# Strassen's method in the down product of an MLP: seven products of quadrants for eight

## The chip, the cores and the metric

One core of one Trainium2 chip. The program is a single launch of one kernel; the metric is its device time in microseconds, and the times shown are those of whole executions. The kernel before took 2549.54, 2552.10 and 2552.34 us in three runs, median 2552.1 us. A profile was taken of one more execution.

## The reference

The reference is two transformer blocks one after the other, for 1024 tokens of width 1024, all in float32. The first block is a mixer (gated convolution and retention), a cross attention on 256 memory rows, and an MLP with a squared ReLU; the second has its own modulation vectors, a windowed attention with a short convolution, and a layer of 16 experts. The change concerns the MLP of the first block:

```python
def sq_relu_mlp(h, up_w, down_w):
    return jnp.square(jax.nn.relu(h @ up_w)) @ down_w     # (1024x1024 @ 1024x4096), then @ 4096x1024
...
h = h + sq_relu_mlp(rmsnorm(h, norm_mlp_w), mlp_up_w, mlp_down_w)
return rmsnorm(h, norm_f_w).astype(x.dtype)
```

and, because it fills gaps in the same stage, the modulation of the second block, `silu(c) @ w_ada + b_ada`: two rows (`c`, and `c_ctx` for a third of the columns) times a 1024x6144 matrix.

## The kernel before

Every large product is made of three matmuls: each float32 operand is split into a high part, rounded to the matmul's own float32r format, and a low part, the difference, and high x high, high x low and low x high are added up in PSUM (`mm3`, L143 to L145). A weight unit is 128x1024 (512 KB). `wunits` (L129) loads it from HBM into one of three `raw` buffers, and `split` (L117) has ScalarE copy the high part (L118) and VectorE subtract the low part (L119) into one of five `W` buffers. These loads and splits are written with a high priority, 1500 instructions ahead of their place.

The framework orders the instructions of each engine when the kernel is built: the written order ranks them, `high_priority` moves a rank forward, and an instruction whose operands come later by the framework's own estimate is passed over for one further back. The result is a fixed queue per engine, which the engine then works off in order, with semaphores between the engines. A tile with a tag (`R16`, `T6`, `W2`, `B4`) can be taken only when all readers of the tile before it with that tag are done.

The MLP (L771 on) runs over nine chunks of the 4096 hidden columns, of 2, 2 and seven times 4 blocks of 128 columns (`MLP_CHUNKS`). In a chunk, each up block is computed for both halves of 512 tokens (`fm_block`, 8 x 3 matmuls of 128x512 into one PSUM bank), ScalarE applies `relu` and `square`, and VectorE makes the high part (a cast) and the low part of `uT`. Then the down product of the chunk: for each of two column halves `nb` and eight token tiles `t`, `tm_block` adds up 4 x 3 matmuls in one of five banks (`pm`), and VectorE adds the bank to `acc[t]`, which holds the residual in SBUF (L801). The units of the down weights, four to a chunk, are the quadrants of its 512x1024 block: 256 rows by 512 columns each.

`mod_blocks` (L760) computes the modulation on VectorE: each of 48 blocks loads 512 KB of `w_ada` into the single buffer R32 and multiplies and sums it against rows of `crow` that are kept in T4 to T7, in two operations, or in four for the first 16 blocks, which use the rows in T6 and T7 as well. Eight blocks are written after each of the chunks 1 to 6. After the MLP, R32 takes `norm_f_w` (`wf`, L819), the sums are added to `modT` (L822), and the eight tiles of `acc` are normalised, tile by tile in the order in which the last chunk finishes them.

Of the kernel before, what the change touches and what calls it, by code (L numbers as in the profile page):

```python
# [11 lines left out]
F32R = mybir.dt.float32r  # L12
# [3 lines left out]
AF = mybir.ActivationFunctionType  # L16
# [2 lines left out]

EPS = 1e-6  # L20
MLP_CHUNKS = [2, 2] + [4] * 7
D = 1024
S = 1024
HALF = 512
# [10 lines left out]
def tile_kernel(ctx: ExitStack, tc: tile.TileContext, d, out, stop=None, dbg=None):  # L35
    nc = tc.nc
    pe, act, dve, pool = nc.tensor, nc.scalar, nc.vector, nc.gpsimd
# [3 lines left out]
    sb = ctx.enter_context(tc.tile_pool(name="sb", bufs=1))  # L41
# [12 lines left out]
    def nm(s):  # L54
        cnt[0] += 1
        return f"{s}_{cnt[0]}"
# [3 lines left out]
    def R(i, shape, dt=F32, name="r"):  # L60
        return sb.tile(shape, dt, tag=f"R{i}", bufs=1, name=nm(name))

    def T(i, shape, dt=F32, name="t"):
        return sb.tile(shape, dt, tag=f"T{i}", bufs=1, name=nm(name))

    def B(i, name="b"):
        return ps[0].tile([128, 512], F32, tag=f"B{i}", bufs=1, name=nm(name))
# [49 lines left out]
    def split(hi, lo, src):  # L117
        act.activation(hi, src, AF.Copy)  # L118
        dve.tensor_sub(lo, src, hi.bitcast(F32))  # L119

    raw_ring = [Ring([("raw", i) for i in range(3)])]
    w_ring = [Ring(range(5))]

    def raw_unit(src):
        pre, i = raw_ring[0]()
        raw = sb.tile([128, 1024], F32, tag=f"{pre}{i}", bufs=1, name=nm("raw"))
        nc.sync.dma_start(raw, src)
        return raw

    def wunits(src, i0, n, ahead=1500):  # L130

        res = []
        with tc.high_priority(offset=ahead):
            for u in range(i0, i0 + n):
                raw = raw_unit(src[u])
                w = sb.tile([128, 2, 1024], F32R, tag=f"W{w_ring[0]()}", bufs=1, name=nm("w"))
                split(w[:, 0, :], w[:, 1, :], raw)
                res.append(w)
        return res
# [18 lines left out]
    def fm_block(p, unit, rhs, n=512):  # L158

        for k in range(8):  # L160
            mm3(p[:, :n], (unit[:, 0, k * 128:(k + 1) * 128], unit[:, 1, k * 128:(k + 1) * 128]),
                rhs(k), k == 0, k == 7)
# [26 lines left out]
    def row_rstd(x):  # L189
        return rsqrt_of(sumsq(x), 1.0 / D)  # L190

# [6 lines left out]
    def unit_tiles(xs):  # L198
# [3 lines left out]
        for j, x in enumerate(xs):  # L202
            if j % 2 == 0:
                act.activation(junk, x, AF.Square, accum_out=ss[:, j:j + 1])
            else:
                dve.tensor_tensor_reduce(out=junk2, in0=x, in1=x, op0=OP.mult, op1=OP.add, scale=1.0, scalar=0.0,
                                         accum_out=ss[:, j:j + 1])
        r = rsqrt_of(ss, 1.0 / D, n)
        for j, x in enumerate(xs):
# [101 lines left out]
    def half_of(hT, half):  # L311
        def f(k):
            h = hT[half][k]
            return (h[:, 0, :], h[:, 1, :])
        return f

    def rows(t, n=1):
        return slice(t * 128, (t + n) * 128)
# [83 lines left out]
    for c in range(4):  # L402
        ub, ua = wunits(d["w_in_fm"], 2 * c, 2)
        for half in range(2):
            sl = slice(half * HALF, (half + 1) * HALF)
            p = B(pm(), "cb")
# [3 lines left out]
            p = B(pm(), "ca")  # L410
# [20 lines left out]
    uni = wunits(d["w_in_tm"], 4, 4)  # L431
    for t in range(8):
        p = B(pm(), "qk")
# [17 lines left out]
    uni = wunits(d["w_in_tm"], 8, 4)  # L451
# [168 lines left out]
    for h in range(4):  # L620
        uni = wunits(d["xk_fm"], 2 * h, 2)
        p = B(pmem(), "km")
# [5 lines left out]
    for nb in range(2):  # L628
        uni = wunits(d["xv_tm"], 4 * nb, 4)
        for j in range(2):  # L630
            p = B(pmem(), "vm")
# [106 lines left out]
    hm = {}  # L738
# [7 lines left out]
    acc = [load(R(24 + t, [128, 1024], name="acc"), h2_d[rows(t), :]) for t in range(8)]  # L746
# [13 lines left out]
    def mod_blocks(b0, n):  # L760

        for b in range(b0, b0 + n):
            raw = load(R(32, [128, 1024], name="wada"), d["w_ada"][b])
            for o in range(2 if b < 16 else 1):
                for h in range(2):
                    dve.tensor_tensor_reduce(out=mjunk, in0=raw[:, h * 512:(h + 1) * 512], in1=crow[o, h],  # L766
                                             op0=OP.mult, op1=OP.add, scale=1.0, scalar=0.0,
                                             accum_out=mpart[:, h, 48 * o + b:48 * o + b + 1])
# [1 line left out]
    rr = Ring([0, 1])  # L770
    rv = Ring([2, 3])  # L771
    UT = {0: [16, 21, 22, 23], 1: [17, 18, 19, 20]}
    ch0 = 0
    for ch, fbs in enumerate(MLP_CHUNKS):
        uT = {0: [], 1: []}
        for fb in range(fbs):
            uni = wunits(d["up_fm"], ch0 + fb, 1)
            for half in range(2):
                p = B(pm(), "up")
                fm_block(p, uni[0], half_of(hm, half))  # L780
                r = T(rr(), [128, 512], name="relu")
                act.activation(r, p, AF.Relu)  # L782
                v = T(rv(), [128, 512], name="sq")
                act.activation(v, r, AF.Square)
                ut = R(UT[half][fb], [128, 2, 512], F32R, name="uT")
                dve.tensor_copy(ut[:, 0, :], v)
                dve.tensor_sub(ut[:, 1, :], v, ut[:, 0, :].bitcast(F32))  # L787
                uT[half].append(ut)
        nu = fbs // 2
        if ch < 8:  # L790
            order = [(nb, t) for nb in range(2) for t in range(8)]
        else:
            order = [(nb, t) for t in range(8) for nb in range(2)]
        uni = {}
        for nb, t in order:
            if nb not in uni:
                uni[nb] = wunits(d["down_tm"], ch0 + nb * nu, nu)
            sl = slice(nb * 512, (nb + 1) * 512)
            p = B(pm(), "dn")
            tm_block(p, tile_of(uT, t), uni[nb])  # L800
            dve.tensor_add(acc[t][:, sl], p, acc[t][:, sl])  # L801
        ch0 += fbs
        if 1 <= ch < 7:
            mod_blocks(8 * ch - 8, 8)

# [20 lines left out]
    p = B(pt(), "modT")  # L828
# [8 lines left out]
    for t in range(8):  # L837
        x = acc[t]
        dbg_store("h3", (rows(t), slice(0, 1024)), x)
        s1 = sumsq(x)  # L840
        dve.tensor_mul(x, x, wf)
        s2 = sumsq(x)
        r = rsqrt_of(s1, 1.0 / D)
        q2 = tiny([128, 1])
        dve.tensor_mul(q2, r, r)
        dve.tensor_mul(q2, q2, s2)
        r2 = rsqrt_of(q2, 1.0 / D)
        r3 = tiny([128, 1])
# [107 lines left out]
    def attention(t):  # L956
# [16 lines left out]
        for kv in range(2):  # L973
            Pl = []
            for hp in range(2):
# [3 lines left out]
                for jj in range(2):  # L979
                    h = h0 + jj  # L980

                    s2 = ps[0].tile([128, 1024], F32, tag=f"D{jj}", bufs=1, name=nm("s2"))
                    pc, pl, sc = s2[:, 256:512], s2[:, 512:512 + nl], s2[:, 256:512 + nl]
# [54 lines left out]
    for c in range(4):  # L1038
        uni = wunits(d["w_in2_fm"], 3 * c, 3)
        uc = R(16, [128, 1024], name="u2")  # L1040
        yc = R(17, [128, 1024], name="y2")
        for half in range(2):
            sl = slice(half * HALF, (half + 1) * HALF)
            g = T(8, [128, 512], name="cg")
            p = B(pmc(), "cg")
# [3 lines left out]
            p = B(pmc(), "hv")  # L1049
# [8 lines left out]
        for half in range(2):  # L1058
            sl = slice(half * HALF, (half + 1) * HALF)
            p = B(pmc(), "bg")  # L1060
# [19 lines left out]
    p = B(7, "lb")  # L1080
# [103 lines left out]
    p = B(7, "aT")  # L1184
# [7 lines left out]
    src = p[:48, :]  # L1192
    for r in range(16):
        sl = slice(8 * r, 8 * r + 8)
        dve.max(G[:, sl], src)
        dve.max_index(Iu[:, sl], G[:, sl], src)
        if r < 15:
            dve.match_replace(out=aT, in_to_replace=G[:, sl], in_values=src, imm_value=-1.0)
            src = aT
# [8 lines left out]
    p = B(4, "GT")  # L1208
# [28 lines left out]
    for e in range(16):  # L1237
# [3 lines left out]
        for nb in range(2):  # L1241
            sl = slice(nb * 512, (nb + 1) * 512)
# [5 lines left out]
            p = B(pga(), "ga")  # L1248
# [5 lines left out]
            p = B(pga(), "up")  # L1254
# [11 lines left out]
        for nb in range(2):  # L1266
            sl = slice(nb * 512, (nb + 1) * 512)
# [7 lines left out]
    sq = tiny([128, 1])  # L1275
# [6 lines left out]
    for t4 in (0, 4):  # L1282
# [3 lines left out]
        r = rsqrt_of(ss, 1.0 / D, 4)  # L1286
# [3 lines left out]
    with tc.high_priority(offset=1500):  # L1290
        ss = tiny([128, 2])
        for nb in range(2):
            sl = slice(nb * 512, (nb + 1) * 512)
# [67 lines left out]
def layout(inputs):  # L1361
# [34 lines left out]
    chunks, r0 = [], 0  # L1396
    for fbs in MLP_CHUNKS:
        chunks.append(_tm(dn[r0:r0 + fbs * 128], [0, 512]))
# [38 lines left out]
```

## Time and profile before

| | before |
|---|---|
| three runs, us | 2549.54, 2552.10, 2552.34; median 2552.1 |
| the profiled execution, us | 2549.31 |
| its span, us | 2547.5 |
| mean granted TensorE clock | 0.983 |
| TensorE busy, us (share) | 2426.0 (95%) |
| VectorE busy, us (share) | 1774.4 (70%) |
| ScalarE busy, us (share) | 1172.0 (46%) |

The span is the time from the first to the last instruction of the profiled execution. Busy time is the union of an engine's instructions. The matmuls overlap: a 128x512 matmul is shown as 389 ns long, and the distance from one start to the next tells the pace. PE is TensorE, PEld its weight loads, DVE VectorE, ACT ScalarE, SP the engine that issues the loads and stores.

### The profile page before, as it was taken

What the parts mean: (1) busy time and instruction counts of PE and PEld (TensorE: products, weight loads), DVE (VectorE), ACT (ScalarE), POOL (GpSimd) and SP (SyncE); (2) the same over time, 40 slices, a digit from 0 to 9 for tenths busy, and PEclk for the clock granted to TensorE, in tenths of its full rate; (3) what the DMA queues carried; (4) which work ended last, traced back from release to release, by engine and by line L of the source; (5) the groups of instructions that cost most, each with busy time, mean ns of one, the idle gap of its engine ahead of it and who ended that gap; (6) DMA issues with size and microseconds to landing.
All of it is one profiled execution on the core that took longest, in us unless ns stands there. A gap on an engine that the chain in (4) does not pass through costs nothing.

```text
span 2547.5 us, 31406 instructions
## 1 busy us (share of the span) xinstructions
PE 2426.0 (95%) x11471; PEld 1971.0 (77%) x11471; DVE 1774.4 (70%) x3121; ACT 1172.0 (46%) x1791; POOL 56.5 (2%) x37
## 2 busy tenths in 40 slices
PE   7999899999999999999999999999994999999995
PEld 6887678888878888888888777777773888888774
DVE  6999883655477555333335858776558999999887
ACT  6113652544442122112214625554333888887775
POOL 0000000000000000000000000000000100011100
PEclk9999999999999999999999999999996999999998
DMA  4333545434443344211111221114674999999994
GB/s 177 101 127 114 167 162 194 142 99 162 133 166 121 119 149 149 71 42 50 58 49 70 98 79 50 38 54 145 206 268 147 389 396 394 393 394 388 361 375 157
DMA packets 138475, 442.79 MB, mean 174 GB/s; under 512 B 15664, under 2 KB 20176, under 8 KB 138320
## 3 DMA queue, kind: packets, MB, share of 16 engines
q1 hardware_dynamic: 133568, 423.48, 46.7%
q0 software_dynamic: 4752, 17.30, 2.7%
q8 instruction: 90, 1.47, 0.2%
q14 instruction: 65, 0.53, 0.1%
HBM read 388.28 MB, written 52.45 MB: 173 GB/s over the span
## 4 chain that ended last, share of the span: by engine, by line
PE 83%; DVE 7%; DMA 4%; ACT 3%; issue 2%; SPq 0%; DVEq 0%; POOLq 0%; ACTq 0%
PE up L144 6%; PE up L145 6%; PE up L143 6%; PE dn L144 6%; PE dn L145 6%; PE dn L143 6%; PE wo L143 3%; PE wo L144 3%; PE wo L145 3%; PE ga L144 2%; PE ga L145 2%; PE ga L143 2%; PE q L145 2%; PE q L144 2%; PE q L143 2%; DMA raw<-experts 2%
## 5 line engine op out<-in xcount | busy, mean ns | idle before, releaser
L118 ACT ACTIVATE w<-raw 128x1024 fp32r<-128x1024 f32 x560 | 584.6, 1058 | 742.4 <-PE dn L145 290.0
L119 DVE TENSOR_TENSOR w<-raw,w 128x1024 fp32r<-128x1024 f32 x560 | 673.0, 1222 | 183.0 <-ACT w L118 171.5
L143 PE MATMUL dn<-w,uT 128*128 128x512 f32 x512 | 199.6, 390 | 0.7 <-ACT relu L782 0.5
L143 PE MATMUL up<-hm,w 128*128 128x512 f32 x512 | 199.7, 390 | 0.0
L144 PE MATMUL up<-hm,w 128*128 128x512 f32 x512 | 199.4, 390 | 0.0
L145 PE MATMUL up<-hm,w 128*128 128x512 f32 x512 | 199.4, 389 | 0.0
L144 PE MATMUL dn<-w,uT 128*128 128x512 f32 x512 | 199.2, 389 | 0.0
L145 PE MATMUL dn<-w,uT 128*128 128x512 f32 x512 | 198.8, 390 | 0.0
L801 DVE TENSOR_TENSOR acc<-dn,acc 128x512 f32<-128x512 f32 x144 | 97.9, 687 | 91.5 <-PE dn L145 91.1
L766 DVE CUSTOM_DVE_ANT_0 mws<-wada,crow 128x512 bf16<-128x512 f32 x128 | 88.2, 689 | 104.4 <-DMA wada<-w_ada 102.3
L423 DVE SCALAR_TENSOR_TENSOR y<-u,small,y 128x1023 f32<-128x1023 f32 (+25 forms) x120 | 145.8, 1261 | 0.4
L143 PEld LDWEIGHTS dn<-w,uT 128*128 128x128 f32 x512 | 96.1, 188 | 21.8 <-ACT relu L782 1.2
L145 PEld LDWEIGHTS dn<-w,uT 128*128 128x128 f32 x512 | 96.0, 188 | 20.5 <-DVE uT L787 0.6
L145 PEld LDWEIGHTS up<-hm,w 128*128 128x128 f32 x512 | 96.1, 188 | 20.0
L144 PEld LDWEIGHTS up<-hm,w 128*128 128x128 f32 x512 | 96.1, 188 | 19.8
L144 PEld LDWEIGHTS dn<-w,uT 128*128 128x128 f32 x512 | 96.1, 188 | 19.8
L143 PEld LDWEIGHTS up<-hm,w 128*128 128x128 f32 x512 | 96.0, 188 | 19.8 <-ACT hm L228 0.3
L144 PE MATMUL ga<-w,x1T 128*128 128x512 f32 x256 | 101.7, 397 | 1.7 <-DVE w L119 1.7
L144 PE MATMUL dn<-w,x1T 128*128 128x512 f32 x256 | 101.4, 396 | 2.0 <-DVE w L119 2.0
L143 PE MATMUL dn<-w,x1T 128*128 128x512 f32 x256 | 102.4, 401 | 0.5 <-ACT w L118 0.5
L145 PE MATMUL dn<-w,x1T 128*128 128x512 f32 x256 | 101.2, 395 | 0.0
L145 PE MATMUL ga<-w,x1T 128*128 128x512 f32 x256 | 101.1, 395 | 0.0
(435 smaller groups left out, 5453.2 us busy)
## 6 DMA issues: line engine op xcount, KB each, us to landing
raw<-experts SPq DMA_DIRECT2D x384, 512.0 KB, 7.1
wada<-w_ada SPq DMA_DIRECT2D x48, 512.0 KB, 3.5
raw<-up_fm SPq DMA_DIRECT2D x32, 512.0 KB, 4.2
raw<-down_tm SPq DMA_DIRECT2D x32, 512.0 KB, 4.4
raw<-w_out_tm SPq DMA_DIRECT2D x24, 512.0 KB, 4.3
raw<-w_in_fm SPq DMA_DIRECT2D x20, 512.0 KB, 3.9
h_d<-hx SPq DMA_DIRECT2D x32, 256.0 KB, 2.9
raw<-xq_fm SPq DMA_DIRECT2D x16, 512.0 KB, 5.0
```

Source lines behind the costliest of these rows:

```text
L118: act.activation(hi, src, AF.Copy)
L119: dve.tensor_sub(lo, src, hi.bitcast(F32))
L143: pe.matmul(out_, l[0], r[0], start=first, stop=False)
L144: pe.matmul(out_, l[0], r[1], start=False, stop=False)
L145: pe.matmul(out_, l[1], r[0], start=False, stop=last)
L423: dve.scalar_tensor_tensor(yc[:, s:], uc[:, :1024 - s], convw[:, c, 30 - s:31 - s], yc[:, s:], op0=OP.mult, op1=OP.add)
L766: dve.tensor_tensor_reduce(out=mjunk, in0=raw[:, h * 512:(h + 1) * 512], in1=crow[o, h], op0=OP.mult, op1=OP.add, scale=1.0, scalar=0.0, a ...
L801: dve.tensor_add(acc[t][:, sl], p, acc[t][:, sl])
```

## The change

The six chunks 2 to 7 no longer multiply the four quadrants of their activations (512 tokens by 256 hidden columns each) with the four quadrants of their down weights in eight products, but form seven products of sums and differences of quadrants, in Winograd's variant of Strassen's method. Each product is 512x256 times 256x512: four banks of six matmuls. The sums that several results share are not formed again: a product is added in PSUM to the four banks that hold the one before, and VectorE adds the banks to `acc` at each stage of their growth, four adds to a quadrant of the result; there are seven such groups of four.

The chunks 0, 1 and 8 keep the old form, which moves into a function `mlp_chunk`. In the new `mlp_chunk_7` the up blocks come in two groups of four, with the first product between them. The quadrants of activations and their sums are held in R16 to R23 and in W3 and W4; the ring of weight buffers is cut to three in these chunks. The squares go to T0 to T3 in the first group and to T6 and T7 in the second. The up blocks use the banks 4 to 7, the products banks 0 to 3 (`bA`, `bC`) and 4 to 7 (`bB`). The sums of weight quadrants (T1 to T4 of the method) are formed on VectorE in the raw buffers, in place, ahead of their place by a priority of 1500; the first quadrant of the weights is loaded twice. The modulation blocks are spread anew: eight after each of the chunks 0 and 1, five after each of the chunks 2 to 7, two after the last.

```diff
 MLP_CHUNKS = [2, 2] + [4] * 7
+MOD_BLOCKS = [8, 8] + [5] * 6 + [2]
...
+    pu = Ring([4, 5, 6, 7])
+    def x_place(i, name):
+        if i < 4:
+            return [R(16 + 2 * i + f, [128, 2, 512], F32R, name=name) for f in range(2)]
+        w = sb.tile([128, 2, 2, 512], F32R, tag=f"W{i - 1}", bufs=1, name=nm(name))
+        return [w[:, 0], w[:, 1]]
+    def mlp_chunk_7(ch0):
+        def u_block(unit, half, place):
+            p = B(pu(), "up")
+            fm_block(p, unit, half_of(hm, half))
+            v = T(place, [128, 512], name="sq")
+            act.activation(v, p, AF.Relu)
+            act.activation(v, v, AF.Square)
+            return v
+        def put(op, v):
+            split(op[:, 0, :], op[:, 1, :], v)
...
+        def product(bank, op, w, first):
+            for j in range(4):
+                for f in range(2):
+                    o = f * 512
+                    l0, l1 = op[f][:, 0, rows(j)], op[f][:, 1, rows(j)]
+                    r0, r1 = w[:, 0, o:o + 512], w[:, 1, o:o + 512]
+                    for i, (l, r) in enumerate(((l0, r0), (l0, r1), (l1, r0))):
+                        pe.matmul(bank[j], l, r, start=first and f + i == 0, stop=f == 1 and i == 2,
+                                  skip_group_check=not first)
+        def add(bank, half, nb):
+            sl = slice(nb * 512, (nb + 1) * 512)
+            for j in range(4):
+                a = acc[4 * half + j]
+                dve.tensor_add(a[:, sl], bank[j], a[:, sl])
+        xA, xB = x_place(0, "x11"), x_place(1, "s3")
+        s3, x21 = [], []
+        for f in range(2):
+            uni = wunits(d["up_fm"], ch0 + f, 1)
+            a = u_block(uni[0], 0, 2 * f)
+            put(xA[f], a)
+            b = u_block(uni[0], 1, 2 * f + 1)
+            dve.tensor_sub(a, a, b)
+            put(xB[f], a)
+            s3.append(a)
+            x21.append(b)
+        w = wunits(d["down_tm"], ch0, 1)[0]
+        bA = [B(j, "dnA") for j in range(4)]
+        product(bA, xA, w, True)
+        add(bA, 0, 0)
+        xC, xD, xE, xF, xG = (x_place(i, n) for i, n in ((2, "x22"), (3, "s1"), (4, "s2"), (5, "x12"), (0, "s4")))
+        for f in range(2):
+            uni = wunits(d["up_fm"], ch0 + 2 + f, 1)
+            b = u_block(uni[0], 1, 6)
+            put(xC[f], b)
+            dve.tensor_add(x21[f], x21[f], b)
+            put(xD[f], x21[f])
+            dve.tensor_sub(s3[f], b, s3[f])
+            put(xE[f], s3[f])
+            a = u_block(uni[0], 0, 7)
+            put(xF[f], a)
+            dve.tensor_sub(a, a, s3[f])
+            put(xG[f], a)
...
+        with tc.high_priority(offset=1500):
+            y12, y22, y11 = (raw_unit(d["down_tm"][ch0 + i]) for i in (2, 3, 0))
+            dve.tensor_sub(y11, y12, y11)
+            t1 = wsplit(y11)
+            dve.tensor_sub(y11, y22, y11)
+            t2 = wsplit(y11)
+            dve.tensor_sub(y12, y22, y12)
+            t3 = wsplit(y12)
+        bB = [B(4 + j, "dnB") for j in range(4)]
+        product(bB, xD, t1, True)
+        add(bB, 1, 1)
+        product(bA, xE, t2, False)
+        add(bA, 0, 1)
+        with tc.high_priority(offset=1500):
+            y21 = raw_unit(d["down_tm"][ch0 + 1])
+            dve.tensor_sub(y11, y21, y11)
+            t4 = wsplit(y11)
+            w22 = wsplit(y22)
+            w21 = wsplit(y21)
+        product(bA, xB, t3, False)
+        add(bA, 1, 1)
+        product(bA, xC, t4, False)
+        add(bA, 1, 0)
+        product(bB, xG, w22, False)
+        add(bB, 0, 1)
+        bC = [B(j, "dnC") for j in range(4)]
+        product(bC, xF, w21, True)
+        add(bC, 0, 0)
...
+        if ch == 2:
+            w_ring[0] = Ring(range(3))
+        if ch == len(MLP_CHUNKS) - 1:
+            w_ring[0] = Ring(range(5))
+        if 2 <= ch < len(MLP_CHUNKS) - 1:
+            mlp_chunk_7(ch0)
+        else:
+            mlp_chunk(ch, ch0, fbs, ch == len(MLP_CHUNKS) - 1)
         ch0 += fbs
-        if 1 <= ch < 7:
-            mod_blocks(8 * ch - 8, 8)
+        n = MOD_BLOCKS[ch]
+        mod_blocks(mb, n)
+        mb += n
```

## Rows read from the trace of the kernel before

**Rows 1.** The page: busy time of TensorE, and the chain that ended last.
```profile
PE 2426.0 (95%) x11471; PEld 1971.0 (77%) x11471; DVE 1774.4 (70%) x3121; ACT 1172.0 (46%) x1791; POOL 56.5 (2%) x37
...
PE 83%; DVE 7%; DMA 4%; ACT 3%; issue 2%; SPq 0%; DVEq 0%; POOLq 0%; ACTq 0%
PE up L144 6%; PE up L145 6%; PE up L143 6%; PE dn L144 6%; PE dn L145 6%; PE dn L143 6%; PE wo L143 3%; PE wo L144 3%; PE wo L145 3%; PE ga L144 2%; PE ga L145 2%; PE ga L143 2%; PE q L145 2%; PE q L144 2%; PE q L143 2%; DMA raw<-experts 2%
```

**Rows 2.** Windows: length, busy PE, PEld, DVE, ACT, POOL, clock, DMA share, GB/s.
```profile
703.00:1410.00 707.00, 703.36 (x3118) 580.04 (x3116) 352.98 (x723) 182.93 (x264) 0.00 (x0) 1.00 0.29 94
846.00:1023.00 177.00, 177.00 (x781) 146.24 (x780) 96.55 (x210) 35.77 (x48) 0.00 (x0) 1.00 0.45 143
1040.00:1125.00 85.00, 85.00 (x377) 70.39 (x376) 27.54 (x39) 16.33 (x23) 0.00 (x0) 1.00 0.16 50
...
1958.00:1960.00 2.00, 2.00 (x6) 1.47 (x6) 1.04 (x2) 0.53 (x1) 0.95 (x1) 0.50 1.01 414
```

**Rows 3.** Timeline, ScalarE: start, length, operation [idle before it <- what ended that].
```profile
724.80 0.64 ACT L757 ACTIVATE crow<-crow 128x512 f32<-128x512 f32 x1
...
896.97 1.06 ACT L118 ACTIVATE w<-raw 128x1024 fp32r<-128x1024 f32 x1 [4.17 <-PE up L145]
...
898.55 0.63 ACT L784 ACTIVATE sq<-relu 128x512 f32<-128x512 f32 x1
...
1076.83 0.60 ACT L782 ACTIVATE relu<-up 128x512 f32<-128x512 f32 x1 [3.23 <-PE up L145]
...
1087.71 0.60 ACT L782 ACTIVATE relu<-up 128x512 f32<-128x512 f32 x1 [3.23 <-PE up L145]
```

**Rows 4.** Groups of instructions, 703 to 1410: busy, mean ns | idle before.
```profile
L143 PE MATMUL dn<-w,uT 128*128 128x512 f32 x512 | 199.6, 390 | 0.7 <-ACT relu L782 0.5 <-DVE uT L786 0.2
...
L801 DVE TENSOR_TENSOR acc<-dn,acc 128x512 f32<-128x512 f32 x144 | 97.9, 687 | 91.5 <-PE dn L145 91.1
...
L766 DVE CUSTOM_DVE_ANT_0 mws<-wada,crow 128x512 bf16<-128x512 f32 x127 | 87.5, 689 | 104.4 <-DMA wada<-w_ada 102.3 <-ACT crow L757 0.6
...
L786 DVE CAST uT<-sq 128x512 fp32r<-128x512 f32 x64 | 27.2, 425 | 58.2 <-ACT sq L784 58.2
```

**Rows 5.** The modulation tiles: the sum over all blocks, and a load's landing.
```profile
L822 DVE TENSOR_TENSOR modT<-mws x1: 226/226/226, 1023.1 to 1023.1; 128x64 f32<-128x64 f32 x1
...
DMA to landing us min/median/max: 3.4/3.5/5.6
```

**Rows 6.** Timeline, VectorE, 901 to 908.
```profile
901.21 0.69 DVE L766 CUSTOM_DVE_ANT_0 mws<-wada,crow 128x512 bf16<-128x512 f32 x1 [3.38 <-DMA wada<-w_ada]
...
902.56 1.22 DVE L119 TENSOR_TENSOR w<-raw,w 128x1024 fp32r<-128x1024 f32 x1
...
906.36 0.69 DVE L766 CUSTOM_DVE_ANT_0 mws<-wada,crow 128x512 bf16<-128x512 f32 x1 [2.24 <-DMA wada<-w_ada]
...
906.98 0.69 DVE L787 TENSOR_TENSOR uT<-sq,uT 128x512 fp32r<-128x512 f32 x1
```

**Rows 7.** Waits of VectorE, 846 to 1023: total us, times, longest us.
```profile
DVE mws L766 <- DMA wada<-w_ada: 79.7, 32, 4.0
```

**Rows 8.** Timeline, VectorE: starts of blocks with four operations, and the last one's end.
```profile
814.55 0.69 DVE L766 CUSTOM_DVE_ANT_0 mws<-wada,crow 128x512 bf16<-128x512 f32 x1 [1.22 <-DMA wada<-w_ada]
...
821.01 0.69 DVE L766 CUSTOM_DVE_ANT_0 mws<-wada,crow 128x512 bf16<-128x512 f32 x1 [2.49 <-DMA wada<-w_ada]
...
843.30 0.69 DVE L766 CUSTOM_DVE_ANT_0 mws<-wada,crow 128x512 bf16<-128x512 f32 x1 [3.25 <-DMA wada<-w_ada]
...
846.13 0.08 DVE L766 DVE_READ_ACCUMULATOR2_ANT mws<- 128x1 f32 x1
```

**Rows 9.** Timeline, TensorE: the first matmul of chunk 2, and two at half clock.
```profile
798.86 0.39 PE L143 MATMUL up<-hm,w 128*128 128x512 f32 x1
...
1958.69 0.63 PE L145 MATMUL ga<-w,x1T 128*128 128x512 f32 x1
1959.12 0.63 PE L143 MATMUL ga<-w,x1T 128*128 128x512 f32 x1
```

More of the change, by code (lines that the diff above doesn't have):

```diff
@@ L772, in tile_kernel, with mlp_chunk @@
     UT = {0: [16, 21, 22, 23], 1: [17, 18, 19, 20]}
-    ch0 = 0
-    for ch, fbs in enumerate(MLP_CHUNKS):
+    def mlp_chunk(ch, ch0, fbs, last):
         uT = {0: [], 1: []}
@@ L789, in tile_kernel @@
         nu = fbs // 2
-        if ch < 8:
+        if not last:
             order = [(nb, t) for nb in range(2) for t in range(8)]
@@ L801, in tile_kernel, with w_place, wsplit @@
             dve.tensor_add(acc[t][:, sl], p, acc[t][:, sl])
+    pu = Ring([4, 5, 6, 7])
[14 more added lines that the diff above has]
+            split(op[:, 0, :], op[:, 1, :], v)
+        def w_place():
+            return sb.tile([128, 2, 1024], F32R, tag=f"W{w_ring[0]()}", bufs=1, name=nm("w"))
+        def product(bank, op, w, first):
[40 more added lines that the diff above has]
+            put(xG[f], a)
+        def wsplit(src):
+            w = w_place()
+            split(w[:, 0, :], w[:, 1, :], src)
+            return w
+        with tc.high_priority(offset=1500):
[26 more added lines that the diff above has]
+        add(bC, 0, 0)
@@ L802, in tile_kernel @@
+    ch0 = 0
+    mb = 0
+    for ch, fbs in enumerate(MLP_CHUNKS):
+        if ch == 2:
[6 more added lines that the diff above has]
+            mlp_chunk(ch, ch0, fbs, ch == len(MLP_CHUNKS) - 1)
         ch0 += fbs
-        if 1 <= ch < 7:
-            mod_blocks(8 * ch - 8, 8)
+        n = MOD_BLOCKS[ch]
+        mod_blocks(mb, n)
+        mb += n
```

## The prediction

> **What bounds the kernel now.** Read the page first: TensorE is busy 95% of the span and supplies 83% of the chain that ended last, and the up and down products of this MLP alone are 36% of that chain [rows 1]. Next cut out the stage. From 703 to 1410 us, TensorE is busy 703 of 707 us at a granted clock of 1.00, VectorE about half of that and ScalarE a quarter; between 1040 and 1125, where no modulation blocks run, VectorE works 27.5 of 85 us [rows 2]. A full bar is not yet a bound, so look at the pace: the `relu` of one up block starts 10.88 us after that of the block two before it, which is 48 matmuls, so 0.2267 us from matmul to matmul with nothing between [rows 3]. The groups of instructions of that stage show 0.7 us of idle time before its matmuls, all of it in front of the down product [rows 4]. So TensorE is the stage, and what shortens its queue shortens the span one for one, as long as it stays fed.
>
> The Trainium skill would have one doubt the full bar: "Perfetto Trace Analysis", section on the most contended engine, calls matmul busy time a bad metric and goes by weight loading, which is 82% here. By that rule up to a fifth of the time could be slack, and the matmuls removed would give back 82% of their time, about 27 us instead of 33; the even pace above shows no slack, and I go by it.
>
> **What is removed.** A chunk of four up blocks has a down product of 16 bank groups of 12 matmuls, 192. Seven products of 24 are 168. Six chunks times 24 is 144 matmuls, times 0.2267 us: **32.6 us less for TensorE**. The up blocks stay (192 a chunk), so a chunk goes from 87.1 to 81.6 us. The matmuls keep their shape, so I see no reason for another pace; the end below is 32.6 saved, the end above is nothing saved if TensorE waits that time instead.
>
> **What is added on VectorE.** Durations from [rows 3, 4, 6]. Before, a chunk had 8 weight splits (1.22), 8 casts and 8 subtractions for uT (0.425, 0.691) and 16 adds into acc (0.687): 9.8 + 8.9 + 11.0 = 29.7 us. After: 11 splits and 4 differences of weight units, 15 x 1.22 = 18.3; 14 low parts and 8 sums of 128x512, 22 x 0.69 = 15.2 (nearest row: the uT subtraction, same shape and type); 28 adds out of PSUM, 19.2. Sum **52.7 of 81.6 us**. ScalarE: 11 weight copies of 1.06, relu and square 8 x 1.22, 14 high parts at about 0.63: 30 us. A fifth 512 KB load of the down weights per chunk falls into a stage whose DMA share is 0.16 to 0.45 [rows 2]. All of it runs beside TensorE, so on totals it costs nothing; if the cover went, it would cost up to 23 us a chunk on VectorE. ScalarE's 30 us and the load have two thirds of a chunk to hide in; I take nothing for them.
>
> The modulation blocks come on top: two ops of 0.69 plus two reads of the accumulator of 0.08 each, 1.54 us (twice that for the first 16). They are written after the chunks, but are taken up wherever VectorE is free: the sum over them, written after the last chunk, ran at 1023 [rows 5]. With five blocks a chunk VectorE stands at 60 of 81.6 us; with ten, 68.
>
> **Where TensorE can be made to wait.** The old down product cycled five banks and could let an add lag. The new chain has four hand-offs a chunk. (1) First product: needs the split of the third up block, with one block (5.44 us) as cover; relu, square, copy, subtraction are 2.5 us. (2) Product on `s1`: needs x22, a sum and its split from the seventh block; relu, square, sum, copy, subtraction and the gaps are some 4 us, cover 5.44 + 0.68. In the 21.8 us of that second up phase VectorE has 16 ops of 0.69, four adds, and the splits and difference of T1 and T2: 17.5 us, 80% full. (3, 4) The products on `s3` and `x22` write into the banks of the product just before, which VectorE must read first. Between a bank's last matmul of one product and the first of the next lie 18 matmuls, 4.08 us; less the add, 3.4 us of slack. In one product (5.44 us) VectorE has four adds and a split, 4.0 us, in some a weight difference too, 5.2. So by itself each hand-off fits, with 2 to 3.4 us to spare, and in the chunks without modulation I take 0. The other hand-offs have a whole product more.
>
> What does not fit is a VectorE that stands still. Its queue runs in order. In [rows 3, 6] a modulation op waits 3.4 and then 2.2 us for its weights; the weight split that ScalarE had prepared at 898.0 comes at 902.6, and the uT whose square ended at 899.2 is done at 907.7, 8 us late. In 846 to 1023 there were 32 such waits, 79.7 us, 2.5 us each; VectorE had 96.6 us of work and stood for practically all the rest [rows 2, 7]. Before, no one noticed; after 1023 there are none. Price after: one block in front of a hand-off delays it by 2.5 + 1.5 = 4.0 us against 3.4 of slack, 0.6 us; four hand-offs, 2.4 a chunk; 32 blocks at seven to ten a chunk last about four chunks: **9.6 us lost**. Bounds: nothing, if denser work between two blocks lets each load land in time (it needs 3.5 us [rows 5]); and at worst the whole lag of 8 us less 3.4, 4.6 us at each of 24 hand-offs, 110 us. I take the mean wait, being the row that 32 instances stand behind.
>
> **A gate at the start.** The second up phase squares into T6 and T7, which hold half of `crow`, read by the first 16 modulation blocks. Before, the last four-op block ran at 843.3 to 846.1 [rows 8]. Chunk 2 begins at 798.9 [rows 9]; four up blocks, the first product and one block later, at 831.5, its relu wants T6. If the blocks are no earlier, it waits until 845.5; T6 is used twice in turn, so `s1` is ready some 8 us after, 853.5, against TensorE's arrival at 847.6 + 0.7: 5 us once. But blocks 0 to 15 are now written one chunk sooner, and four-op blocks have followed each other in 6.5 us (814.6 to 821.0, [rows 8]): from the last crow row, done at 725.4 [rows 3], that gives 830 and no wait. I take **2 us**, bounds 0 and 5.
>
> The weight ring of three and the raw ring of three: each slot is freed by the unit three places before, so at least two products (10.9 us) lie between a slot's release and its use, against 1.06 + 1.22 for a split and 3.5 to 5.6 for a load of this size [rows 3, 5, 6]: nothing.
>
> **Sum.** -32.6 + 9.6 + 2 = -21.0 us. The profiled execution took 2549.3 us, its span 2547.5; the median of the three runs is 2552.1, 2.8 higher, and I put the difference on the median: **2531 us**.
>
> **Rivals.**
> *All of it arrives.* Denser VectorE work hides the loads; nothing waits. 2552.1 - 32.6 = 2519.5. For it: TensorE's 0.7 us before, although VectorE stood still 80 us. Against: the new slack is smaller than the lags behind [rows 6]. Chance 0.15.
> *The tail pays.* Blocks 46 and 47 are now written behind the last chunk and share R32 with `norm_f_w`, which each tile's final work needs. If VectorE takes them up only there, that work, now beside the last down product, comes after it: per tile two passes over 128x1024 at up to 1.22 [rows 6] and some 14 one-column ops of at least 0.08 [rows 8], 3.6 us; six of the eight tiles were hidden before, 21 us: 2531 + 21 = 2552, no change. Against: before, all blocks were done at 1023, 387 us ahead of the stage's end [rows 5]. Chance 0.04.
> *Slower: VectorE's standing waits become the chain's pace.* Place: products 3 and 4 and the two product starts, chunks 2 to 7. A product stage has 5.44 us; with four adds, a split and a difference, 5.2, one block with its wait, 4.0, makes 9.2: 3.8 us over. At two such stages and two late starts (4.6 each) in four chunks: 4 x 16.8 = 67 us, 2552.1 - 32.6 + 67 = 2587. It decides from 5.4 us lost per chunk over six chunks. For it: VectorE fully taken in 846 to 1023. Against: the blocks are the lowest in rank and get in only where VectorE has nothing ready. A mild form that eats the gain and no more has 0.07, the slower one 0.06.
> *Slower: the clock.* All rows of this stage have 1.00; at 1958, after TensorE had been almost idle, it was 0.50, 1.2 instead of 2.4 GHz, and matmuls followed at 0.43 us [rows 2, 9]. If short waits brought that on, each matmul at the lower level would cost 0.2 us, and from 27 of them per chunk the gain is gone; all 168 would be 200 us, 2720. Against: no wait I foresee is longer than 5 us. The Trainium skill's "TensorE: Matmul & The Clock Gate", section on PSUM-queue depth-cycling, says that a kernel cycling through banks idles briefly between groups often enough for the clock to swing; the old down product cycles five banks at 1.00 throughout, so the trace does not bear it out here. Chance 0.02.
>
> **The numbers.** Forecast case (5 to 31 us saved): 0.66. Two runs of this kernel tell a difference above 0.2%, 5.1 us. Faster: 0.66 + 0.15 = 0.81. Same: 0.04 + 0.07 = 0.11. Slower: 0.08. Range: from 2518 (all saved, with the runs' scatter of 1.5) to 2548, where 4 us are saved.
>
> **What would show it.** The down product's matmuls fall by 144, pace 0.2267. TensorE's waits in the stage, 0.7 us before, rise to some 10, on the subtraction of `s1` and on the acc adds, in the chunks with modulation blocks and not after. VectorE's wait for `wada` falls below 102 us, its busy time in the stage rises by 6 x 23 = 138. A waiting relu at about 832 shows the gate. Wrong would be: waits of TensorE also in the chunks without blocks, weight splits late, a clock below 1.00, or a modT after 1300.

## The result, and the profile after

Four executions of the changed kernel took 2524.90 to 2529.21 us, median **2526.23 us**, beside 2552.22 us for the kernel before on the same chip: ratio 0.9898, 95% interval 0.9885 to 0.9910. Timed again beside the experiments, it was 2529.91 us beside 2552.07, 22.2 us less: 0.9909 [0.9894, 0.9925]. The forecast was 2531.

The profiled execution took 2526.58 us, its span 2524.8 (before 2549.31 and 2547.5). The page answers [rows 1]: 144 matmuls fewer, and 28.8 us less of busy TensorE. Line numbers after are 1 or 2 higher than before up to the end of the old form, and 121 higher behind the new one (L822, the sum into `modT`, is L943): L119 and L120 are the two halves of a split, L767 the modulation, L839 the products, L846 their adds into `acc`.

```profile
PE 2397.2 (95%) x11327; PEld 1944.9 (77%) x11327; DVE 1899.9 (75%) x3271; ACT 1242.7 (49%) x1893; POOL 56.5 (2%) x37
...
PE 76%; DVE 12%; DMA 7%; ACT 3%; issue 2%; SPq 0%; DVEq 0%; POOLq 0%; ACTq 0%
```

The part of the span outside this stage varies by a few us from one execution to the next, so from here on I go by the stage's own length: from its first up matmul to the transpose of `modT` behind its last product. That is 705.31 us before and **683.98** after, 21.3 less. The first up matmul of the chunks 2 to 6 on TensorE's timeline (start, length, operation) cuts it into chunks:

```profile
799.28 0.39 PE L144 MATMUL up<-hm,w 128*128 128x512 f32 x1
...
889.72 0.39 PE L144 MATMUL up<-hm,w 128*128 128x512 f32 x1
...
972.27 0.39 PE L144 MATMUL up<-hm,w 128*128 128x512 f32 x1
...
1054.67 0.39 PE L144 MATMUL up<-hm,w 128*128 128x512 f32 x1
...
1136.27 0.39 PE L144 MATMUL up<-hm,w 128*128 128x512 f32 x1
```

So chunk 2 took 90.44 us, chunks 3 and 4 82.55 and 82.40, chunk 5 81.60, and so did 6 and 7; before, each took 87.04 (one 87.38). 81.60 is 360 matmuls at 0.2267: the new chunk at its best is 5.44 shorter, exactly 24 matmuls. The windows (columns as in [rows 2]) show the stage, chunk 2, a clean chunk and ten microseconds inside chunk 2:

```profile
703.00:1387.00 684.00, 673.81 (x2960) 553.57 (x2960) 476.94 (x871) 251.71 (x364) 0.00 (x0) 1.00 0.33 102
799.00:890.00 91.00, 85.05 (x364) 68.59 (x364) 71.74 (x139) 27.65 (x41) 0.00 (x0) 0.98 0.36 110
1136.00:1218.00 82.00, 82.00 (x363) 67.92 (x363) 49.92 (x65) 29.86 (x41) 0.00 (x0) 1.00 0.19 59
850.00:860.00 10.00, 7.40 (x24) 5.38 (x25) 9.41 (x19) 8.30 (x16) 0.00 (x0) 0.83 0.46 140
```

In the clean chunk TensorE is full while VectorE works 49.9 us (27.5 of 85 in [rows 2]). In chunk 2 TensorE is idle for 6 us. The groups of the stage, as [rows 4] had them, say who was late:

```profile
L767 DVE CUSTOM_DVE_ANT_0 mws<-wada,crow 128x512 bf16<-128x512 f32 x127 | 87.3, 688 | 52.4 <-DMA wada<-w_ada 50.5 <-ACT crow L758 0.4
L839 PE MATMUL dnB<-w,s 128*128 128x512 f32 x288 | 69.9, 398 | 6.0 <-ACT s L119 4.2 <-ACT w L119 1.1 <-DVE w L120 0.6
L839 PE MATMUL dnA<-w,s 128*128 128x512 f32 x288 | 67.3, 390 | 1.1 <-DVE acc L846 1.1
...
L846 DVE TENSOR_TENSOR acc<-dnA,acc 128x512 f32<-128x512 f32 x96 | 63.1, 684 | 9.8 <-PE dnA L839 9.3
...
L821 ACT ACTIVATE sq<-up 128x512 f32<-128x512 f32 x48 | 28.2, 586 | 69.8 <-PE up L146 59.4 <-DVE mws L767 10.4
```

The products waited 7.1 us, most of it in front of `dnB` for the high part of `s1`; and one relu waited 10.4 us for the modulation. Both are one event, on the timeline of the three engines:

```profile
847.28 0.69 DVE L767 CUSTOM_DVE_ANT_0 mws<-wada,crow 128x512 bf16<-128x512 f32 x1 [2.71 <-DMA wada<-w_ada]
...
849.48 0.69 DVE L767 CUSTOM_DVE_ANT_0 mws<-wada,crow 128x512 bf16<-128x512 f32 x1
850.10 0.08 DVE L767 DVE_READ_ACCUMULATOR2_ANT mws<- 128x1 f32 x1
...
849.48 0.60 ACT L821 ACTIVATE sq<-up 128x512 f32<-128x512 f32 x1 [10.40 <-DVE mws L767]
...
852.31 4.00 PE L839 MATMUL dnB<-w,s 128*128 128x512 f32 x9 [3.91 <-ACT s L119]
856.15 2.92 PE L839 MATMUL dnA<-w,s 128*128 128x512 f32 x12
859.35 3.01 PE L839 MATMUL dnB<-w,s 128*128 128x512 f32 x12 [0.29 <-ACT s L119]
```

The relu writes T6, which holds a row of `crow` until the last block with four operations has read it. That block ran at 847.3 to 850.2 here (843.3 to 846.2 in [rows 8]). The `s1` of the second half starts from this relu, and TensorE, at the end of its up blocks, found it missing. The nine matmuls behind that wait are 0.43 us apart (852.31 to 856.15) instead of 0.23, 1.8 us more; the granted clock of the window 850 to 860 is 0.83. In chunks 3 and 4 another, smaller wait is left, the same in both; here chunk 3:

```profile
944.19 0.68 DVE L767 CUSTOM_DVE_ANT_0 mws<-wada,crow 128x512 bf16<-128x512 f32 x1
...
946.07 1.22 DVE L897 TENSOR_TENSOR raw<-raw,raw 128x1024 f32<-128x1024 f32 x1 [1.19 <-DMA raw<-down_tm]
...
949.62 2.48 DVE L846 TENSOR_TENSOR acc<-dnA,acc 128x512 f32<-128x512 f32 x4
...
950.36 5.75 PE L839 MATMUL dnA<-w,s 128*128 128x512 f32 x24 [0.64 <-DVE acc L846]
```

This is the product on `s3`, which writes into the banks of the product on `s2`. By the pace, an estimate, the first of those banks was ready at 945.5, but VectorE read the first at 949.6: in front of it stood a modulation op, a wait for down weights, a difference, two splits and an add of the group before.

The waits for modulation rows, 102.3 us in [rows 4], are 50.5; `modT` is summed at 1076.4 (1023.1 in [rows 5]); in the chunks after it TensorE waits for nothing.

```profile
L943 DVE TENSOR_TENSOR modT<-mws x1: 226/226/226, 1076.4 to 1076.4; 128x64 f32<-128x64 f32 x1
```

### The profile page after: what moved, and what is told of

Its sections match the earlier page's. It is cut to its first block, busy times and chain, and to the rows that moved or that the text cites. A ratio compares the mean times of both kernels' runs of the same rounds, so it can differ in the third digit from the quotient of the medians.

```text
span 2524.8 us, 31357 instructions
## 1 busy us (share of the span) xinstructions
PE 2397.2 (95%) x11327; PEld 1944.9 (77%) x11327; DVE 1899.9 (75%) x3271; ACT 1242.7 (49%) x1893; POOL 56.5 (2%) x37
## 4 chain that ended last, share of the span: by engine, by line
PE 76%; DVE 12%; DMA 7%; ACT 3%; issue 2%; SPq 0%; DVEq 0%; POOLq 0%; ACTq 0%
PE up L145 6%; PE up L146 6%; PE up L144 6%; PE dnA L839 4%; PE wo L144 3%; PE wo L145 3%; PE wo L146 3%; DVE w L120 2%; PE ga L145 2%; PE ga L146 2%; PE ga L144 2%; PE dnB L839 2%; DMA wada<-w_ada 2%; PE dn L145 2%; PE dn L144 2%
## 5 line engine op out<-in xcount | busy, mean ns | idle before, releaser
L119 ACT ACTIVATE w<-raw 128x1024 fp32r<-128x1024 f32 x578 | 603.4, 1058 | 614.4 <-PE up L146 107.3
L120 DVE TENSOR_TENSOR w<-raw,w 128x1024 fp32r<-128x1024 f32 x578 | 694.8, 1222 | 166.3 <-ACT w L119 154.7
L767 DVE CUSTOM_DVE_ANT_0 mws<-wada,crow 128x512 bf16<-128x512 f32 x128 | 88.0, 688 | 52.4 <-DMA wada<-w_ada 50.5
L145 PE MATMUL ga<-w,x1T 128*128 128x512 f32 x256 | 101.7, 397 | 1.7 <-DVE w L120 1.7
L146 PE MATMUL ga<-w,x1T 128*128 128x512 f32 x256 | 101.1, 395 | 0.0
L145 PE MATMUL up<-w,x1T 128*128 128x512 f32 x256 | 100.9, 394 | 0.2 <-DVE w L120 0.2
L144 PE MATMUL ga<-w,x1T 128*128 128x512 f32 x256 | 100.5, 393 | 0.0
L146 PE MATMUL up<-w,x1T 128*128 128x512 f32 x256 | 99.9, 390 | 0.0
L144 PE MATMUL up<-w,x1T 128*128 128x512 f32 x256 | 99.8, 390 | 0.0
L839 PE MATMUL dnB<-w,s 128*128 128x512 f32 x288 | 69.9, 398 | 6.0 <-ACT s L119 4.2
L1353 POOL DMA_INDIRECT xs<-hf_d,IT x16 | 19.8, 1236 | 2267.1 <-DVE IT L1340 1927.7
L846 DVE TENSOR_TENSOR acc<-dnA,acc 128x512 f32<-128x512 f32 x96 | 63.1, 684 | 9.8 <-PE dnA L839 9.3
```

The source lines that it names most:

```text
L144: pe.matmul(out_, l[0], r[0], start=first, stop=False)
L145: pe.matmul(out_, l[0], r[1], start=False, stop=False)
L146: pe.matmul(out_, l[1], r[0], start=False, stop=last)
L839: pe.matmul(bank[j], l, r, start=first and f + i == 0, stop=f == 1 and i == 2, skip_group_check=not first)
L846: dve.tensor_add(a[:, sl], bank[j], a[:, sl])
L1353: nc.gpsimd.indirect_dma_start(out=xs, out_offset=None, in_=hf_d, in_offset=bass.IndirectOffsetOnAxis(ap=IT[:, e:e + 1], axis=0))
```

## The experiments

The theory at this point: the seven products do save 5.44 us in each of six chunks; 8.8 are given back once, in chunk 2, because squares and `crow` rows share T6 and T7, and 1.8 in chunks 3 and 4 to VectorE's backlog. Rivals: chunk 2 loses to VectorE's amount of work there, or to a start of its own that the first new chunk would pay without any modulation; or the in-order waits for rows are of no account at all.

Medians and ratios to the kernel before on the same chip; stage and chunks from the profiled execution of each. From e4 on, each edit is shown on top of e2's.

| kernel | median us | ratio [95%] | stage | chunk 2 | 3 | 4 | 5 to 7 |
|---|---|---|---|---|---|---|---|
| before | 2552.22 | 1 | 705.31 | 87.03 | 87.04 | 87.38 | 87.04 |
| the change | 2526.23 | 0.9898 [0.9885, 0.9910] | 683.98 | 90.44 | 82.55 | 82.40 | 81.60 |
| after_again | 2529.91 | 0.9909 [0.9894, 0.9925] | 684.92 | 90.71 | 82.41 | 82.27 | 81.60 |
| e1, rows of T4, T5 | 2522.32 | 0.9884 [0.9869, 0.9899] | 677.07 | 83.43 | 82.31 | 82.44 | 81.60 |
| e2, other places | 2526.19 | 0.9904 [0.9889, 0.9919] | 678.36 | 86.46 | 82.49 | 82.33 | 81.60 |
| e3, chunk 2 as before | 2535.16 | 0.9935 [0.9922, 0.9949] | 690.37 | 88.27 | 90.19 | 82.24 | 81.60 |
| e4, e2 and blocks written later | 2524.49 | 0.9884 [0.9867, 0.9901] | 676.65 | 83.99 | 82.35 | 82.55 | 81.60 |
| e5, e2 without blocks | 2527.12 | 0.9896 [0.9879, 0.9912] | 672.93 | 81.60 | 81.60 | 81.60 | 81.60 |
| e6, e2 and 28 ops more | 2535.56 | 0.9933 [0.9916, 0.9949] | 685.23 | 89.16 | 82.50 | 82.51 | 82.48 |
| e7, e2 and blocks first | 2534.22 | 0.9928 [0.9911, 0.9945] | 686.25 | 89.22 | 86.11 | 82.48 | 81.60 |
| e8, e2 and no block written before chunk 3 | 2521.00 | 0.9869 [0.9852, 0.9885] | 676.77 | 83.50 | 82.35 | 82.34 | 81.60 |

**after_again** is the change, unedited.

> The changed kernel once more, to stand beside the others of this set. Expected 2526 us (23 to 29 below the kernel before); chunk 2 of its MLP 90.4 us long, the chunks 5 to 7 81.6 each, as in its first profile.

Chunk lengths come back within 0.3 us; so differences of a chunk by a microsecond mean something, which totals cannot show. The stage is less even: its part ahead of chunk 2 took 95.0 to 97.6 us in these profiles (95.7 before), so a difference of two stages below 2.5 us says nothing.

**e1_same_rows: the blocks use the rows in T4 and T5 alone**; the rows for T6 and T7 are not loaded.

```diff
-    for o in range(2):
+    for o in range(1):
...
-                    dve.tensor_tensor_reduce(..., in1=crow[o, h],
+                    dve.tensor_tensor_reduce(..., in1=crow[0, h],
```

> The modulation blocks 0 to 15 read the rows of T4 and T5 for both outputs, and the rows in T6 and T7 are not loaded: the modulation of the context is left out, every operation on VectorE stays. Theory A (the 8.8 us that chunk 2 is longer than 81.6 come from the squares of its second up phase waiting for T6 and T7, which the last of the 16 blocks releases): chunk 2 falls to 82 to 83 us, ScalarE's 10.4 us wait for the modulation is gone, the whole 7.5 to 9 us faster than the changed kernel, about 2518. Rival B (chunk 2 is long because VectorE is behind with blocks of four operations and their loads): chunk 2 stays near 90 us, 2526.

Chunk 2 fell from 90.44 to 83.43, a little above theory A's range, with the same blocks, operations and loads of `w_ada`. No relu waits for a block, and TensorE's waits in chunks 2 to 4 are adds alone (view of waits, 795 to 1060: total, times, longest):

```profile
PE dnA L839 <- DVE acc L846: 2.5, 3, 1.5
```

So 7.0 of the 8.8 us go with the rows in the two shared tiles. That is not the price of the shared place alone: the edit also loads two rows fewer, the blocks ran earlier, and the last with four operations ended 43.8 us into chunk 2 (50.9 in the change).

**e2_other_places: the squares of the second group in R17, R21 and T1**, which no block of the modulation holds; nothing is left out.

```diff
-            b = u_block(uni[0], 1, 6)
+            b = u_block(uni[0], 1, 17)
+            xC.append(R(20 + f, [128, 2, 512], F32R, name="x22"))
...
-            a = u_block(uni[0], 0, 7)
+            a = u_block(uni[0], 0, 21 if f == 0 else 1)
```

> Nothing left out: the squares of the second up phase go to R17, R21 and T1, which are free at that time in every chunk, instead of T6 and T7. Theory A: the gate is gone, chunk 2 at 82 to 83 us, 2518. Rival B: chunk 2 stays near 90 us, 2526. A third way: R17 and R21 are wanted soon after for x22 and s4, and a new wait of 1 to 3 us in every chunk takes the gain back, 2520 to 2530.

Chunk 2 fell to 86.46 only. The relu no longer waits, but the blocks, free to run, stand between the steps that make `s1`:

```profile
849.19 0.68 DVE L767 CUSTOM_DVE_ANT_0 mws<-wada,crow 128x512 bf16<-128x512 f32 x1
...
850.40 0.68 DVE L767 CUSTOM_DVE_ANT_0 mws<-wada,crow 128x512 bf16<-128x512 f32 x1
...
851.01 0.69 DVE L120 TENSOR_TENSOR s<-sq,s 128x512 fp32r<-128x512 f32 x1
...
849.98 0.73 PE L839 MATMUL dnB<-w,s 128*128 128x512 f32 x2 [0.83 <-ACT s L119]
851.75 6.21 PE L839 MATMUL dnB<-w,s 128*128 128x512 f32 x19 [1.03 <-DVE s L120]
...
850.00:860.00 10.00, 8.97 (x31) 6.94 (x32) 8.66 (x17) 3.89 (x6) 0.00 (x0) 0.83 0.32 107
```

Of the 8.8 us, taking away the shared place alone gives 4.0. Of the 4.9 left, some 2.4 lie around the two waits for `s1`, 1.6 in eight matmuls 0.43 us apart behind them (the last line is the window 850 to 860, its clock 0.83), and 0.8 at the product on `s3`. All of it goes with the blocks: in e5 nothing of it is left.

**e3_five_chunks: chunk 2 in the old form**, so that the blocks are done with T6 and T7 before the first new chunk.

```diff
-        if ch == 2:
+        if ch == 3:
             w_ring[0] = Ring(range(3))
...
-        if 2 <= ch < len(MLP_CHUNKS) - 1:
+        if 3 <= ch < len(MLP_CHUNKS) - 1:
```

> Chunk 2 keeps the old form, chunks 3 to 7 the new. By theory A and 5.44 us per chunk: one chunk's saving less, 8.8 us of gate less, 3.4 us faster than the changed kernel, 2523; no wait for T6. If instead a chunk saved less than 5.44 and the gate were cheaper, it would come out slower than the changed kernel, 2528 or more.

This missed: 2535.16. The number is that of the expectation's second case, 2528 or more, but not for its reason: chunks 5 to 7 save their 5.44 here too. Where the ring of weight buffers is cut to three, the first up unit of chunk 3 can be prepared only after the old down product; ScalarE made its high part at 886.0 and 887.4, VectorE's half came late, and TensorE stood 5 us:

```profile
891.38 0.69 DVE L767 CUSTOM_DVE_ANT_0 mws<-wada,crow 128x512 bf16<-128x512 f32 x1 [3.14 <-DMA wada<-w_ada]
...
893.33 1.22 DVE L120 TENSOR_TENSOR w<-raw,w 128x1024 fp32r<-128x1024 f32 x1
...
894.60 0.79 PE L146 MATMUL up<-hm,w 128*128 128x512 f32 x1 [5.05 <-DVE w L120]
895.20 0.63 PE L144 MATMUL up<-hm,w 128*128 128x512 f32 x1
```

The second matmul is 0.63 us long: the clock had fallen (0.66 in the window 890 to 900). So a standing VectorE cost TensorE 5.05 us at one hand-off, more than the 4.6 that the prediction gave as the worst, where that hand-off had no unit ahead.

**e4_low_rank: blocks written eight behind each of the chunks 2 to 7.**

```diff
-MOD_BLOCKS = [8, 8] + [5] * 6 + [2]
+MOD_BLOCKS = [0, 0] + [8] * 6 + [0]
```

> This is the kernel of e2_other_places with the eight modulation blocks of each chunk ranked behind that chunk's own work, in chunks 2 to 7 (none in the first two chunks, as the order before began). Nothing is left out. Theory A (what is left of chunk 2's excess, 86.46 against 81.60, is four-op blocks that the order put into VectorE's s1 chain of the gate): chunk 2 falls to 82 to 83.5 us, the MLP stage from 678.4 to some 674 to 676, and the kernel is 3 to 5 us below e2. Rival (chunk 2 simply has more VectorE work than fits before the first second-half product, whatever its order): chunk 2 stays at 85.5 to 87 and the stage at 677 to 679.

Chunk 2 at 83.99 is half a microsecond above the theory's range and well below the rival's; the stage, 676.65, is just above its range too. TensorE's wait for `s1` is gone; one wait is left in the chunk, 1.8 us in front of the product on `s3`.

**e5_no_blocks: no modulation blocks.**

```diff
-MOD_BLOCKS = [8, 8] + [5] * 6 + [2]
+MOD_BLOCKS = [0] * 9
...
+    dve.memset(mws, 0.0)
```

> The kernel of e2_other_places without the modulation blocks (and so without their row loads): the context modulation is left out, its sums are set to zero. Theory: everything above 81.60 us in chunks 2 to 4 is a price of the blocks, so all six chunks come to 81.6 to 82.0 and the stage to 671 to 673. Rival (the first new chunk costs something of its own, the s1 chain and the gate): chunk 2 stays at 84 or more while chunks 3 and 4 fall to 81.6.

All six chunks take 81.60, as the theory had it, and the rival of a cost of the first new chunk is out. TensorE waits for nothing from chunk 2 on, and VectorE's own work is alike in all (windows in chunks 2 and 3):

```profile
810.00:891.00 81.00, 81.00 (x359) 67.09 (x358) 49.00 (x65) 29.86 (x41) 0.00 (x0) 1.00 0.18 52
891.00:973.00 82.00, 82.00 (x363) 67.89 (x363) 50.41 (x66) 29.86 (x41) 0.00 (x0) 1.00 0.19 58
```

The median doesn't show the 5.4 us gained on e2: its stage began at 711.75 us, those of the other kernels at 701.7 to 706.7. The loss lies far ahead of the MLP: in 300 to 400 us TensorE was busy 89.4 us, in e2 94.2. Its cause stays open.

**e6_more_vector: an idle subtraction behind each of the 28 adds of a new chunk.** It was built on e2, not on the change as its expectation says; chunks 5 to 7 are the same in the two.

```diff
                 dve.tensor_add(a[:, sl], bank[j], a[:, sl])
+                dve.tensor_sub(mjunk, a[:, sl], a[:, sl])
```

> The kernel of the change with one more VectorE subtraction of 512 columns (some 0.69 us, its result not used) behind each of the 28 accumulation adds of a chunk; nothing is left out. VectorE goes from 50 to some 69.5 of 81.6 us in chunks 6 and 7. By the totals it still fits and chunks 6 and 7 stay within 0.5 us of 81.60. By the reading of one product stage (a row block of a product, 24 matmuls or 5.44 us, in which VectorE then has up to eight ops of 0.69 and its weight splits and X sums beside them) it does not: the first buffers come free late and chunks 6 and 7 take 83 to 90 us each.

Neither came: chunks 5 to 7 are 0.88 us longer, and chunk 2 is 2.7 longer than in e2. The 28 ops of 0.69 us are 19 us more on VectorE, and the chunks are no longer clean, since the blocks, lowest in rank, were pushed back and each of the chunks 3 to 7 held five of them. The loss of chunk 5 is at one place, the product on `s3` again (the window of chunk 5, VectorE, and TensorE's wait):

```profile
1136.00:1218.00 82.00, 81.44 (x359) 67.03 (x358) 71.34 (x114) 29.71 (x41) 0.00 (x0) 1.00 0.30 89
...
1186.92 1.23 DVE L120 TENSOR_TENSOR w<-raw,w 128x1024 fp32r<-128x1024 f32 x1 [2.14 <-ACT w L119]
...
1196.49 0.68 DVE L846 TENSOR_TENSOR acc<-dnA,acc 128x512 f32<-128x512 f32 x1
...
1197.23 1.66 PE L839 MATMUL dnA<-w,s 128*128 128x512 f32 x6 [0.56 <-DVE acc L846]
```

VectorE had been idle for 2.14 us up to 1186.9, and from there to the late add it did three of the idle subtractions and no block, so I lay the wait to them. With VectorE busy 87% of the time, one hand-off was late by a little and the others held.

**e7_blocks_first: the blocks ranked 1500 instructions ahead.**

```diff
-        mod_blocks(mb, n)
+        with tc.high_priority(offset=1500):
+            mod_blocks(mb, n)
```

> The kernel of e2_other_places with the modulation blocks ranked ahead of the chunk's other work by a fixed offset; nothing is left out. Theory (in the change the low rank of the blocks is what kept the hand-offs clear of VectorE's waits for rows, and so made the modulation's price 1.75 us in chunks 3 and 4 where 9.6 was forecast): the blocks of each chunk then come in a train at its head, VectorE waits for rows with the chunk's own work queued behind, and the stage grows by 10 to 40 us over e2's 678.4. Rival (product stages ride out such waits whatever the order, since every hand-off has a buffer ahead): the stage stays within 3 us of 678.4.

The stage grew by 7.9 us over e2, 6.5 of it in chunks 2 to 4: less than the theory's range, more than the rival allows. In 800 to 980, chunks 2 and 3, TensorE waits for adds and for weights:

```profile
PE dnA L839 <- DVE acc L846: 3.8, 2, 2.4
PE dnB L839 <- ACT w L119: 3.1, 2, 1.9
```

Behind these waits, none longer than 2.4 us, the granted clock fell twice (0.68 in 860 to 870, 0.83 in 950 to 960); matmuls 0.43 us apart cost some 3.4 us in the two chunks, 1.6 in e2. VectorE's own waits for rows from 795 to 1140 are hardly more than in e2 (30.1 us in 25 against 29.6 in 23). So their place in the queue, not their sum, sets the price.

**e8_after_gate: as e4, with no block written before chunk 3.**

```diff
-MOD_BLOCKS = [8, 8] + [5] * 6 + [2]
+MOD_BLOCKS = [0, 0, 0] + [10] * 4 + [8, 0]
```

> The kernel of e4_low_rank with no modulation block before chunk 3: ten behind the own work of each of the chunks 3 to 6, eight in chunk 7. Nothing is left out. Theory (the excess of chunk 2 is the start gate's, and blocks that meet a chunk without it cost one late accumulation add, 0.4 to 1.0 us): chunk 2 comes to 81.60 to 81.8, chunks 3 to 6 to 82.0 to 82.7 each, the MLP stage to 674.5 to 676.5, and the kernel is level with e4 within what two runs tell apart. Rival (the blocks with four operations cost 2 to 5 us wherever they first run): chunk 3 or 4 comes to 84 to 87 and the stage to 677 or more.

Chunks 3 and 4 came as the theory had them, at 82.35 and 82.34. Chunks 5 and 6 took 81.60, below its 82.0 to 82.7, for the blocks were done by then (the last began at 1068.0), and the stage is just above its range. Chunk 2 missed: 83.50 for 81.60 to 81.8. The reason is in the waits: VectorE waits for modulation rows in 700 to 800 (first line) and in 800 to 882 (second), before any block is written. The framework had pulled the blocks forward, here and in every kernel of the table that has them: the first runs at 700.6 to 705.4. In chunk 2 the hand-off to `s3` paid 1.6 us (third line):

```profile
DVE mws L767 <- DMA wada<-w_ada: 11.9, 5, 4.1
...
DVE mws L767 <- DMA wada<-w_ada: 10.3, 7, 3.7
...
PE dnA L839 <- DVE acc L846: 1.6, 1, 1.6
```

So this run did not test what it was meant to test, the chunk of the gate without blocks; e5 did. Its stage is level with that of e4 (676.77 and 676.65) and 7.2 us below the change. It is the fastest measured here, with nothing left out: 2521.00 us, 0.9869 [0.9852, 0.9885]; the interval of the change begins where this one ends.

## Why the prediction was right

The time fell by 26.0 us where 21 were forecast, the stage by 21.3. Of the three terms one was exact. The gate was under-sized by 2.1 and the modulation over-sized by 3.1, and that these two errors cancel is luck. The experiments part them better than the chunks do: what e2 gives back in chunks 2 to 4 is the gate's, what e5 gives back after that is the modulation's, in this order of removal.

| term | forecast | stage measured |
|---|---|---|
| 144 matmuls | -32.6 | -32.6 (81.60 for 87.04, six times) |
| gate at T6, T7 | +2 | +4.1 (the change less e2) |
| modulation at the hand-offs | +9.6 | +6.5 (e2 less e5: 4.9 + 0.9 + 0.7, chunks 2 to 4) |
| the old form's own loss in one chunk | | -0.3 |
| first and last parts of the stage | | +1.05 |
| sum | -21.0 | -21.3 |

The rest up to 26 is scatter outside the stage (in the profiled spans, 22.7 in all, it is 1.4; timed again, the time fell by 22.2).

*What is removed.* Held to the hundredth. The Trainium skill, "Perfetto Trace Analysis", section on the most contended engine, judges TensorE's headroom by the share of its peak rate and by weight-load busy time. By the estimate that the forecast made from the second, a clean chunk would have shrunk by some 4.5 us, to 82.6; it shrank by 5.44, so the trace does not bear that estimate out here.

*VectorE's load.* 49.9 of 82 us in a clean chunk for the 52.7 forecast, ScalarE 30 for 30: ops at their old durations (adds 684 ns, splits 1223). That totals hide it was right: clean chunks lost nothing. One sum was short: the splits and differences of T1 and T2 are four ops, so the second up phase comes to 18.7 us by the forecast's own durations, not 17.5.

*Gate at the start: the step that failed.* The prediction saw the wait and its place, and bounded it at 5 us. It took the last block with four operations at 830 to 846, since the blocks were written a chunk sooner and could follow each other in 6.5 us from 725.4 on. Written sooner did not make it run sooner. Before, the first eight blocks were written behind chunk 1 and the next eight behind chunk 2, and the first ran at 701.34 all the same, the tenth at 799.87; after, they ran at 701.23 and 801.71 (two lines of each trace, before first):

```profile
701.34 0.68 DVE L766 CUSTOM_DVE_ANT_0 mws<-wada,crow 128x512 bf16<-128x512 f32 x1
...
799.87 0.69 DVE L766 CUSTOM_DVE_ANT_0 mws<-wada,crow 128x512 bf16<-128x512 f32 x1
...
701.23 0.68 DVE L767 CUSTOM_DVE_ANT_0 mws<-wada,crow 128x512 bf16<-128x512 f32 x1
...
801.71 0.69 DVE L767 CUSTOM_DVE_ANT_0 mws<-wada,crow 128x512 bf16<-128x512 f32 x1 [1.85 <-DMA wada<-w_ada]
```

Nor were they 6.5 us apart: from the second block (735.05) to the last (843.30) the trace before has 7.7 on average. The last ended at 850.2. And chunk 2 lost more than the wait of 3.9 us: three smaller ones behind it, and 1.8 us to matmuls at the lowered clock. e2 puts the shared place at 4.1 us, inside the bounds and twice the size taken; the rest of chunk 2 is the modulation's.

*Modulation at the hand-offs: over-sized by 3.1, and elsewhere than forecast.* Four late hand-offs in four chunks were forecast, 0.6 us each. With the gate gone (e2), 4.9 of the 6.5 us fall in chunk 2, most of it at the product on `s1`, and 1.6 of that is the clock, which the forecast's sum left out; chunks 3 and 4 have one late hand-off each, 0.9 and 0.7 (0.95 and 0.80 in the change). Denser work between two blocks let the loads land in time (waits of 1.1 us each in 890 to 1055, 15.4 us in 14, for the 2.5 of [rows 7]). That denser work is the reason is argued, not shown; it is the one that the prediction gave for its lower bound.

*Rivals.* "All of it arrives" describes chunks 5 to 7 and, without blocks, all. "VectorE's standing waits" is a true mechanism, seen in e3 and e7, and the low rank of the blocks, named against it, kept it smaller: ranked ahead they cost 6.5 us more in chunks 2 to 4. The tail never paid: `modT` was summed 310 us ahead of the stage's end. The clock fell once in the six chunks, behind the longest wait (0.83 in 850 to 860), and cost 1.8 us.

## What to carry to other kernels

A matmul taken off a full TensorE comes back at its pace, to the hundredth, wherever every hand-off is met; so price each hand-off by its place in the queue of the engine that serves it, not by that engine's total. Where a new tile shares a tag with a long-lived one, find in the trace where the last reader of the old tile runs, not where the order of writing puts it, and follow everything that hangs behind the waiting instruction. And compare stages cut at fixed instructions: chunk lengths came back within 0.3 us where whole executions differ by 4.

## What the runs showed that I had not expected

Waits of a few microseconds, some of one, were followed by the lower clock, and so cost more than their length. Behind 3.91 us without a matmul, nine matmuls of the change are 0.43 us apart, the pace of the lower level in [rows 9]. In e3, behind 5.05 us, the matmul rows are 0.63 us long and 0.43 apart, before they are 0.39 long and 0.23 apart again: eight matmuls, 1.6 us on top of the wait. But e2 shows the same behind two waits of 0.83 and 1.03 us, and e7 twice where none was longer than 2.4, while a wait of 1.8 us in chunk 2 of e4 left the clock at 1.00. What tells these cases apart no run here shows. The forecast had seen the lower level only where TensorE had been almost idle [rows 9], and had set against it that no wait would be longer than 5 us; that was no guard.
